# Loading two neighbouring input chunks by one transfer in a convolution with max pooling

## The chip, the core and the metric

The kernel runs on one core of a Trainium2 chip. The core has five engines that run side by side: TensorE (PE, matrix products), VectorE (DVE), ScalarE (ACT), GpSimd (POOL) and SyncE (SP, which in this kernel issues transfers and does no arithmetic). Sixteen DMA engines move data between the chip's large memory and the core's own memory; a transfer is issued by one instruction on SP, ACT or POOL, and raises a semaphore when it has landed. The metric is the device time of one execution in microseconds (us).

## The reference: a 3x3 convolution and a 2x2 maximum

The input `x` holds 16 images of 64 channels and 64 x 64 pixels, the weight is 128 x 64 x 3 x 3, everything in 32-bit floats. With the border padded by zeros:

```
conv[b, co, i, j] = sum over ci, kh, kw of weight[co, ci, kh, kw] * x_pad[b, ci, i+kh, j+kw]
output[b, co, i, j] = max of conv[b, co, 2i:2i+2, 2j:2j+2]
```

The output is 16 x 128 x 32 x 32.

## The kernel before

**Tiling.** Two images make a pair: their 64 channels each fill the 128 partitions. There are eight pairs, and each pair's 64 rows are cut into four chunks of 16 rows (eight pairs of rows, which is what the pooling takes together). That makes 32 chunks. The string `SEQ` gives each chunk one of two ways of being computed:

- 13 K chunks (names with `k`, and the step names in capitals): their input is loaded by POOL's queue, cast to bf16 on the way (`kload`, line 105, tile `kx`). One helper row tile `ks` is made for a chunk.
- 19 W chunks (names with `w`, step names in small letters): their input is loaded as 32-bit floats by SP's queue (`wload`, line 113) into one of three buffers `wx` that hold a whole pair of images each. From it four row tiles of sums and differences of rows are made on DVE and POOL by `row_op` (line 260): `we`, `ws`, `wz`, `wy`, steps `E`/`e`, `S`, `Z`, `Y`.

The matrix products (line 202) read `kx` and the row tiles and add into eight PSUM banks `acc`. ACT copies or negates banks (`ev` line 290, seeding line 295, `od` line 303), DVE takes the maxima (`acc` line 299, `o` line 327), and the finished chunk `o` of both images is stored from SP's queue (line 344). For the last two chunks the halves are stored one by one (lines 342 and 320), and of the last two such halves ACT issues one and SP the other (`flush_late`).

**Where chunks lie.** Chunks W16, W17 and W18 are the second, third and fourth quarter of the last pair of images; the first quarter of that pair is the last K chunk. All three lie in the buffer `wx_1`, which W4 to W7 have used before: W16 in its rows 15 to 32 of the image, W17 in rows 33 to 48, W18 in rows 49 to 63.

**Order.** Nothing is scheduled by a program: the string `ORDER` (lines 420 to 477) is the issue order, read from left to right, and each engine executes its own instructions in that order. `LD.16`, `LD.17` and `LD.18` are the loads of the three chunks. `LD.16` and `LD.17` stand on line 454; `LD.18` stands ten lines further on, on line 464, ahead of `e.17`. The steps that read W17's rows are `e.17` (POOL), `S.17` (DVE), `Z.17` and `Y.17`; those that read W18's are `S.18`, `e.18`, `Y.18`, `Z.18`. `L4` on line 453 is a K load on POOL's queue that is in flight beside `LD.16` and `LD.17`. SP executes loads and stores in the same order, so a store that waits for its data holds up every later transfer of SP.

**Semaphores.** The transfers issued by SP and ACT take eight semaphores in turn, the first transfer the first of them, the ninth the first again, and so on. There are 57 such transfers, so the last one, the store of line 320 on SP, takes the first semaphore, and the store of line 320 on ACT, one before it in the order, takes the eighth. At the end of the program SP waits for the eight semaphores one after the other, from the first to the eighth; these instructions, and the barrier of all engines behind them, show under line 543.

Of the kernel before, what the change touches and what calls it, by code (L numbers as in the profile page):

```python
# [10 lines left out]
def kernel(  # L11
# [31 lines left out]
    place = {}  # L43
    number = {}
    for c in SEQ.lower():
        i = sum(1 for g in place if g[0] == c)
        j, q = divmod(i, NQ)
# [25 lines left out]
    def behind(inst, other):  # L73
        if other is not None:
            tc.add_manual_dep(inst.ins, other.ins.name, SYNC, reason="order")
# [9 lines left out]
    def rows_of(p, lo, hi):  # L85
        return x[2 * p : 2 * p + 2].rearrange("b c h w -> (b c) h w")[:, lo:hi, :]

    def chunk(q):
        return (2 * R * q + (q > 0), min(H, 2 * R * (q + 1) + 1))

    kx = {}
    loaded = set()
# [11 lines left out]
        hi = chunk(q + n - 1)[1]  # L104
        return nc.gpsimd.dma_start(out=ktile(i)[:, lo:hi, :], in_=rows_of(p, lo, hi))  # L105

    def wload(i):
        loaded.add(i)
        p, q = place["w", i]
        lo, hi = chunk(q)  # L110
        if i % NQ == 0 and q:
            lo -= 2
        return nc.sync.dma_start(
            out=wx[i // NQ % 3][:, lo + 1 : hi + 1, :], in_=rows_of(p, lo, hi)
        )
# [17 lines left out]
    D2, G0, D0, G2, GM, G1, GP = range(1, 29, 4)  # L133
# [118 lines left out]
    mark = {}  # L252
# [33 lines left out]
    ev, od, ot = {}, {}, {}  # L286
# [80 lines left out]
    def load_second():  # L367
        return nc.sync.dma_start(out=ksecond, in_=rows_of(0, klo2, khi2))

    def load_w(i):  # L370
        behind(wload(i), mark.get({0: "D2", 1: "GM", 2: "E0", 3: "E1"}.get(i)))

    def note(name, inst):
        mark[name] = inst
# [4 lines left out]
    def load_k(n):  # L379
# [21 lines left out]
        "X2": lambda e: cast_more(e, 1),  # L401
        "KX2": lambda: behind(load_second(), mark["D2"]),
        "LD": load_w,
        "L": load_k,
        "KS": lambda i: note(f"KS{i}", ks(i)), "S": ws, "Z": wz, "Y": wy, "SE": seed,
# [6 lines left out]
    for name, f in ("ev", evac), ("mx", rowmax), ("od", odd), ("cm", colmax):  # L412
# [38 lines left out]
        mx.9.1 P2.10.0:2+PR.7.1 SE.10.1:1 cm.7.0 PBb.7.0+P1.9.1 E.11 OD.7.1 P1.9.0+P0.10.1 LD.14 CM.7.1  # L451
        od.9.1 Z.12 MX.7.0 LD.15 PAa.8.0:4+P3.10.1 od.9.0 cm.9.1 ev.10.1 PR.7.0+PAa.8.1:6 S.11 SE.10.0:3
        PAb.8.0+PAb.8.1 Y.11 mx.10.1 OD.7.0 P3.10.0+P2.11.1:0 CM.7.0 EV.8.1 cm.9.0 P0.10.0+P1.10.1 L4 KS.8
        SE.11.1:6 S.12 PBa.8.0:7+PBa.8.1:5 ev.10.0 LD.16 E.12 PBb.8.0+P0.11.1 EV.8.0 LD.17 mx.10.0 od.10.1
        Y.13 P2.11.0:2+PBb.8.1 ev.11.1 MX.8.0 P1.10.0+P3.11.1 SE.11.0:4 cm.10.1 Y.12 PR.8.0+PAa.9.1:0 MX.8.1
        od.10.0 P0.11.0+P2.12.1:1 mx.11.1 OD.8.0 Z.13 cm.10.0 P3.11.0+PR.8.1 ev.11.0 CM.8.0
        P2.12.0:3+P1.11.1 OD.8.1 mx.11.0 e.13 SE.12.1:2 PBa.9.0:7+PAb.9.1 CM.8.1 od.11.1 P1.11.0+P3.12.1
# [3 lines left out]
        CM.9.1 OD.9.0 Y.15 ev.13.1 CM.9.0 P1.13.0+P2.14.1:0 od.12.1 mx.13.1 od.12.0 PAa.11.0:4+P2.15.1:5  # L461
        od.13.0 Z.15 cm.12.0 SE.14.1:7 PAb.11.0+P1.13.1 cm.12.1 cm.13.0 PAa.10.0:6+P0.14.1 od.13.1 E.16
        SE.15.1:1 PAb.10.0+P3.14.1 S.15 ev.14.1 P2.14.0:2+P0.15.1 EV.11.0 cm.13.1 S.14 L5 P2.15.0:0+P3.15.1
        ev.15.1 LD.18 e.17 mx.14.1 PBa.10.0:4+PAa.11.1:3 EV.10.0 mx.15.1 SE.14.0:5 PBb.10.0+PAb.11.1
        SE.15.0:6 S.17 P0.14.0+P1.14.1 EV.11.1 KS.10 P0.15.0+P1.15.1 Z.17 MX.10.0 ev.14.0 P3.15.0+PAa.10.1:3
        od.15.1 ev.15.0 cm.15.1 P3.14.0+PAb.10.1 Y.16 od.14.1 mx.15.0 PR.10.0+PBa.10.1:2 EV.10.1 mx.14.0
        Y.17 P2.17.0:0+PBb.10.1 OD.10.0 cm.14.1 P1.15.0+P2.16.1:3 SE.17.0:1 MX.10.1 Z.16 P1.14.0+PAa.12.1:7
# [12 lines left out]
    for n in range(8):  # L480
        src = zeros if n > 5 else ones
        warm = nc.tensor.matmul(  # L482
            acc[:, n], src[:, 0:128], src, start=True, stop=True, skip_group_check=True
        )
        if n == 3:
            behind(load_second() if SEQ[1] == "K" else wload(0), warm)
# [6 lines left out]
    for s in ORDER.split():  # L493
        act_left[0] -= on_act(s)
        if s[0] == "P":
            made = []
            for p in s.split("+"):
                p, _, bank = p.partition(":")
                n, i, h = p.split(".")
# [48 lines left out]
```

## Time and profile before

| | us |
|---|---|
| time, median of 3 runs | 105.21 |
| lowest and highest | 104.98, 105.22 |
| time of the profiled execution | 104.99 |
| its span, first to last instruction | 103.1 |
| PE busy | 97.3 (94%) |
| DVE busy | 90.4 (88%) |
| ACT busy | 81.8 (79%) |
| POOL busy | 67.2 (65%) |

Times inside the profile are counted from the start of the span. A name with a small q (SPq, POOLq, ACTq) is an engine's instruction sequencer: it issues transfers and waits for semaphores, and is not counted as busy. "DMA to landing" is the time from the issue of a transfer until its semaphore is complete. In rows of instructions the three durations are minimum, median and maximum in nanoseconds, and behind them stands when the first and the last instruction started. The time lies 1.9 us above the span in the profiled execution (104.99 - 103.1).

### The profile page before, as it was taken

How to read it: one execution, taken by the hardware profiler on the slowest of the kernel's cores; microseconds unless marked ns; L12 is line 12 of the kernel's file. 1: busy time of each engine (PE TensorE's matmuls, PEld its weight loads, DVE VectorE, ACT ScalarE, POOL GpSimd, SP SyncE). 2: the span in 40 equal slices, each digit the busy share in tenths (PEclk: the TensorE clock that was granted, in tenths of full speed). 3: DMA queues.
4: the chain of work that ended last, by engine and by line, in shares of the span. 5: the costliest groups of instructions: out<-in, count | busy, mean ns of one | idle time of the engine just before them, and what ended most of it. 6: DMA issues, size and time to landing. Idle time of an engine off the chain costs nothing.

```text
span 103.1 us, 2507 instructions
## 1 busy us (share of the span) xinstructions
PE 97.3 (94%) x888; PEld 57.3 (56%) x888; DVE 90.4 (88%) x178; ACT 81.8 (79%) x177; POOL 67.2 (65%) x76
## 2 busy tenths in 40 slices
PE   6998999999999999999999999999999999999920
PEld 2273555555765555655555665665555656666500
DVE  1599979998898898897998999989999999989950
ACT  4478987787988867799879988889889988988630
POOL 7306679847958769967795856993992697580000
PEclk9999999999999999999999999999999999999999
DMA  2987988899998996689899788999947921512362
GB/s 52 366 287 246 211 174 284 208 302 224 373 354 283 153 231 261 227 216 147 189 284 416 269 189 301 270 217 267 358 155 154 244 114 68 197 43 97 108 230 79
DMA packets 12925, 22.81 MB, mean 221 GB/s; under 512 B 1008, under 2 KB 9200, under 8 KB 12912
## 3 DMA queue, kind: packets, MB, share of 16 engines
q1 hardware_dynamic: 11904, 19.63, 57.5%
q0 software_dynamic: 864, 2.88, 19.2%
q8 instruction: 7, 0.11, 0.5%
q10 hardware_dynamic: 144, 0.13, 0.4%
q14 instruction: 6, 0.05, 0.1%
HBM read 17.14 MB, written 8.39 MB: 248 GB/s over the span
## 4 chain that ended last, share of the span: by engine, by line
PE 81%; DMA 7%; DVE 5%; issue 1%; ACT 1%
PE acc L202 81%; DMA ksecond<-in_x_dram 5%; DMA wraw<-in_weight_dram 3%; DVE acc L299 2%; DVE o L327 2%; DVE wq L391 1%; ACT kx L348 1%; DVE wq L356 0%
## 5 line engine op out<-in xcount | busy, mean ns | idle before, releaser
L202 PEld LDWEIGHTS <-wt 64*128 64x128 bf16 x852 | 54.6, 94 | 36.8 <-issue 0.6
L202 PE MATMUL acc<-kx,wt 64*128 64x504 bf16 (+5 forms) x318 | 57.5, 369 | 0.3 <-ACT kx L348 0.3
L299 DVE TENSOR_TENSOR acc<-acc,ev 128x512 f32<-128x512 f32 x64 | 42.4, 692 | 3.1 <-PE acc L202 2.0
L290 ACT COPY ev<-acc 128x512 f32<-128x512 f32 x64 | 36.6, 592 | 6.2 <-PE acc L202 5.5
L260 POOL TENSOR_TENSOR wz<-wx 128x512 bf16<-128x512 f32 x19 | 24.2, 1275 | 10.6 <-DVE ks L260 4.3
L202 PE MATMUL acc<-wy,wt 64*128 64x504 bf16 (+1 forms) x114 | 29.6, 377 | 0.0
L260 POOL TENSOR_TENSOR wy<-wx 128x512 bf16<-128x512 f32 x19 | 24.1, 1273 | 7.8 <-PE acc L202 3.1
L202 PE MATMUL acc<-wz,wt 64*128 64x504 bf16 (+1 forms) x114 | 29.2, 377 | 0.0
L202 PE MATMUL acc<-we,wt 64*128 64x504 bf16 (+1 forms) x114 | 29.1, 377 | 0.0
L202 PE MATMUL acc<-ws,wt 64*128 64x504 bf16 (+1 forms) x114 | 29.1, 376 | 0.0
L327 DVE TENSOR_TENSOR o<-acc,od 128x256 f32<-128x256 f32 x64 | 25.2, 417 | 2.3 <-ACT od L303 1.9
L303 ACT COPY od<-acc 128x256 f32<-128x256 f32 x64 | 23.0, 381 | 4.1 <-PE acc L202 3.2
L295 ACT ACTIVATE acc<-acc 128x512 f32<-128x512 f32 x38 | 22.0, 586 | 3.3 <-DVE o L327 1.9
L202 PE MATMUL acc<-ks,wt 64*128 64x504 bf16 (+1 forms) x78 | 19.5, 377 | 0.0
L260 POOL TENSOR_TENSOR we<-wx 128x512 bf16<-128x512 f32 x11 | 14.0, 1271 | 5.1 <-PE acc L202 3.4
L260 DVE TENSOR_TENSOR ws<-wx 128x512 bf16<-128x512 f32 x19 | 15.0, 793 | 0.0
L260 DVE TENSOR_TENSOR we<-wx 128x512 bf16<-128x512 f32 x8 | 6.1, 768 | 0.0
L260 DVE TENSOR_TENSOR ks<-kx 128x512 bf16<-128x512 bf16 x13 | 5.4, 419 | 0.1
L105 POOL DMA_DIRECT2D kx<-in_x_dram x6 | 3.5, 592 | 0.0
L482 PE MATMUL acc<-const-bfloat16-1.0 128*128 128x512 bf16 x6 | 2.7, 623 | 0.8 <-PEq L529 0.8
L356 DVE TENSOR_TENSOR wq<-wraw 128x192 bf16<-128x192 f32 x1 | 0.5, 502 | 2.6 <-DMA wraw<-in_weight_dram 2.6
L164 PEld LDWEIGHTS <-wq 128*128 128x128 bf16 x28 | 1.7, 101 | 1.6 <-issue 0.9
(28 smaller groups left out, 18.5 us busy)
## 6 DMA issues: line engine op xcount, KB each, us to landing
out_dram<-o SPq DMA_DIRECT2D x30, 256.0 KB, 4.7
wx<-in_x_dram SPq DMA_DIRECT2D x9, 512.0 KB, 7.2
wx<-in_x_dram SPq DMA_DIRECT2D x5, 480.0 KB, 6.0
wx<-in_x_dram SPq DMA_DIRECT2D x4, 544.0 KB, 6.6
kx<-in_x_dram POOLq DMA_DIRECT2D x3, 496.0 KB, 8.0
kx<-in_x_dram POOLq DMA_DIRECT2D x2, 528.0 KB, 8.6
wx<-in_x_dram SPq DMA_DIRECT2D x1, 576.0 KB, 9.7
ksecond<-in_x_dram SPq DMA_DIRECT2D x1, 512.0 KB, 4.7
```

The source lines that it names most:

```text
L105: return nc.gpsimd.dma_start(out=ktile(i)[:, lo:hi, :], in_=rows_of(p, lo, hi))
L164: nc.tensor.transpose(turned_rows(m)[:, j, :], wq[:, BLOCKS[m] - 1 + j : BLOCKS[m] + 1 + j, :].rearrange("a b c -> a (b c)"), ident,)
L202: lambda kw=kw, o0=o0, o1=o1, c0=c0, c1=c1: nc.tensor.matmul(dst[:, i0:i1, o0:o1], wt[lo : lo + CI, m0 + kw - h, :], rows(lo, i0, i1, c0, c1),
L260: return engine.tensor_tensor(out=r, in0=t[:, f + a : f + a + 2 * R - 1 : 2, :], in1=t[:, f + b : f + b + 2 * R - 1 : 2, :], op=op,)
L290: nc.scalar.copy(out=ev[g], in_=acc[:, ta[g]])
L295: nc.scalar.mul(acc[:, t], acc[:, ta["w", i, h]], -1.0)
L299: nc.vector.tensor_tensor(out=t, in0=t, in1=ev.pop(g), op=MAX)
L303: nc.scalar.copy(out=od[g], in_=acc[:, tb[g], :, 1::2])
L327: nc.vector.tensor_tensor(out=o[:, h], in0=acc[:, tb[g], :, 0::2], in1=od.pop(g), op=MAX,)
L348: nc.scalar.copy(out=out, in_=in_)
L391: "D2", on_vector(nc.vector.tensor_sub(out=slots(D2), in0=g2, in1=g1))
L482: warm = nc.tensor.matmul(acc[:, n], src[:, 0:128], src, start=True, stop=True, skip_group_check=True)
```

## The change

`wload` and the step `LD` take a second number, how many neighbouring chunks of one pair of images are to be loaded by one transfer. `LD.17` becomes `LD.17.2`: one transfer of rows 33 to 63, 992 KB, 7936 bytes in each partition, at the place of the old `LD.17`. `LD.18` is taken out of its place on line 464. The instructions of PE, DVE, ACT and POOL stay as they are and in their order. On SP and ACT 56 transfers are left in place of 57, and each transfer that follows the removed one takes the semaphore before the one that it had; the last store takes the eighth in place of the first, and the last store of ACT the seventh in place of the eighth.

```diff
-    def wload(i):
-        loaded.add(i)
+    def wload(i, n=1):
+        loaded.update(range(i, i + n))
         p, q = place["w", i]
-        lo, hi = chunk(q)
+        assert place["w", i + n - 1] == (p, q + n - 1)
+        lo, hi = chunk(q)[0], chunk(q + n - 1)[1]
         if i % NQ == 0 and q:
             lo -= 2
         return nc.sync.dma_start(
...
-    def load_w(i):
-        behind(wload(i), mark.get({0: "D2", 1: "GM", 2: "E0", 3: "E1"}.get(i)))
+    def load_w(i, n=1):
+        behind(wload(i, n), mark.get({0: "D2", 1: "GM", 2: "E0", 3: "E1"}.get(i)))
...
-        SE.11.1:6 S.12 PBa.8.0:7+PBa.8.1:5 ev.10.0 LD.16 E.12 PBb.8.0+P0.11.1 EV.8.0 LD.17 mx.10.0 od.10.1
+        SE.11.1:6 S.12 PBa.8.0:7+PBa.8.1:5 ev.10.0 LD.16 E.12 PBb.8.0+P0.11.1 EV.8.0 LD.17.2 mx.10.0 od.10.1
...
-        ev.15.1 LD.18 e.17 mx.14.1 PBa.10.0:4+PAa.11.1:3 EV.10.0 mx.15.1 SE.14.0:5 PBb.10.0+PAb.11.1
+        ev.15.1 e.17 mx.14.1 PBa.10.0:4+PAa.11.1:3 EV.10.0 mx.15.1 SE.14.0:5 PBb.10.0+PAb.11.1
```

## The prediction

> **What bounds the kernel now.** I read the page first, then the chain that ended last, then who waited for whom on PE and SP, then the end of the program, and last the transfers that the change touches.
>
> ```profile
> span 103.1 us, 2507 instructions
> PE 97.3 (94%) x888; PEld 57.3 (56%) x888; DVE 90.4 (88%) x178; ACT 81.8 (79%) x177; POOL 67.2 (65%) x76
> ```
>
> The chain that ended last (start, duration, what), its long middle and its end:
>
> ```profile
> 10.36 83.77 PE acc L202 x772
> 94.12 0.60 DVE acc L299
> ...
> 98.38 1.09 DVE o L327 x3
> ```
>
> PE runs without a break for 83.8 us and sets the pace from 10.4 to 94.1 us. Behind it comes a tail of DVE and stores. In the middle, time can be lost only by something that makes PE wait, and PE hardly waits: the only wait of its products is 0.3 us in total.
>
> ```profile
> PE acc L202 <- ACT kx L348: 0.3, 1, 0.3
> ```
>
> So a transfer that comes earlier can bring nothing there, and one that comes later costs something only when it comes later than its first reader. The tail is another matter: each instruction there stands on the path. The last stores, and what SP then waits for:
>
> ```profile
> L342 SPq DMA_DIRECT2D out_dram<-o x2: 408/413/418, 98.6 to 99.1; - x2
> ...
> L320 ACTq DMA_DIRECT2D out_dram<-o x1: 372/372/372, 99.2 to 99.2; - x1
> L320 SPq DMA_DIRECT2D out_dram<-o x1: 407/407/407, 99.6 to 99.6; - x1
> ...
> DMA to landing us min/median/max: 2.1/2.2/2.2
> ```
>
> ```profile
> SPq L344 <- DVE o L327: 62.3, 26, 6.3
> ...
> SPq L543 <- DMA out_dram<-o: 1.8, 1, 1.8
> ```
>
> The last store is issued at 99.6 and lands 2.2 us later, at 101.8. SP's waits show one wait of 1.8 us on line 543 for a store, 100.0 to 101.8, and no second one. The rows of SP's semaphore instructions on line 543 tell which of the eight that was; the first row takes the stretch 101.7 to 102.3, the second 101.81 to 101.82, the third 102.24 to 102.25, the fourth 102.3 to 102.33:
>
> ```profile
> L543 SPq EVENT_SEMAPHORE  x8: 17/28/28, 101.8 to 102.2; - x8
> ...
> L543 SPq EVENT_SEMAPHORE  x1: 17/17/17, 101.8 to 101.8; - x1
> ...
> L543 SPq EVENT_SEMAPHORE  x1: 28/28/28, 102.2 to 102.2; - x1
> ...
> L543 SPq DRAIN  x1: 7/7/7, 102.3 to 102.3; - x1
> ```
>
> All eight waits start after the last landing: the first of them is the one that the last store held up, and the seven others, long fulfilled, are worked off one by one behind it. From the first to the eighth it takes 0.42 to 0.44 us, some 62 ns for each of seven steps. Only then does SP drain and let the final barrier begin. Nothing else is late there.
>
> **The change, part by part.**
>
> *The last store's semaphore.* One transfer fewer stands ahead of it, so the rotation of eight moves back by one: the last store takes the eighth semaphore, ACT's store the seventh. The order of the end waits stays. SP is then through with issuing at 100.0 (99.6 + 0.4); the stores of line 342 land by 101.3 (99.1 + 2.2) and ACT's at 101.4 (99.2 + 2.2), so the first seven waits are worked off before the last landing at 101.8, with 0.3 us to spare after the seventh (101.4 + 0.06 = 101.5). At 101.8 the eighth alone is left. The steps from first to eighth, 7 x 62 ns = 0.43 us, leave the path and nothing fills the place: drain and barrier come 0.43 us earlier. Bounds: if only the 28 ns that each row records counted without a profiler, 7 x 0.028 = 0.20; from the first wait to the drain it is 0.50 (102.31 - 101.81), and more cannot go. I take 0.43, what this stretch itself measures.
>
> [...]
>
> *The merged load.* The old loads W16 and W17, then W18 (issue, and time to landing), with the rate at which W17 ran out:
>
> ```profile
> L113 SPq DMA_DIRECT2D wx<-in_x_dram x2: 446/598/751, 63.5 to 64.1; - x2
> ...
> DMA to landing us min/median/max: 9.7/10.0/10.3
> ```
>
> ```profile
> L113 SPq DMA_DIRECT2D wx<-in_x_dram x1: 468/468/468, 79.5 to 79.5; - x1
> ...
> DMA to landing us min/median/max: 5.0/5.0/5.0
> ```
>
> ```profile
> 72.00:74.00 2.00, 2.00 (x21) 1.14 (x18) 2.00 (x5) 1.76 (x4) 2.00 (x3) 1.00 1.01 375
> ```
>
> W17 landed at 74.4 (64.1 + 10.3). The 480 KB of W18 now ride with it. At the 375 GB/s of 72 to 74 us, where the DMA engines are full (share 1.01), 0.492 MB take 1.3 us; the other end is the whole 5.0 us that W18 took by itself. The merged transfer lands at 75.7, at the latest at 79.4. I take 75.7, since it follows W17 in the same queue without a new issue. A gain against 74.4 is excluded: there are more bytes in front of the same semaphore. First readers: POOL's `we` for W17, DVE's `ws` for W18; the first two rows below are DVE's `we` for W16 and the first product that reads the K load of step L4.
>
> ```profile
> 76.91 1.20 DVE L260 TENSOR_TENSOR we<-wx 128x512 bf16<-128x512 f32 x1
> ```
>
> ```profile
> L202 PE MATMUL acc<-kx,wt x7: 376/377/377, 75.5 to 76.8; 64*128 64x504 bf16 x4, 64*128 64x512 bf16 x3
> ```
>
> ```profile
> 79.88 1.26 POOL L260 TENSOR_TENSOR we<-wx 128x512 bf16<-128x512 f32 x1 [1.81 <-PE acc L202]
> ```
>
> ```profile
> 86.83 0.79 DVE L260 TENSOR_TENSOR ws<-wx 128x512 bf16<-128x512 f32 x1
> ```
>
> POOL's `we` starts at 79.88, and until then it waited for PE (a row buffer), not for the load. Cover 5.5 us, of which 1.3 are used; even 5.0 fit. `ws` of W18 starts at 86.83 with no idle time before it, so the old landing at 84.5 (79.5 + 5.0) cost nothing and the earlier one brings nothing. W16 stands ahead of the merged transfer in its queue and doesn't move. Cost: 0.
>
> *Stores behind it on SP.* The three stores issued at 67.5 to 71.5 stand in the same queue behind the merged transfer and land 1.3 us later (5.0 at most).
>
> ```profile
> L344 SPq DMA_DIRECT2D out_dram<-o x3: 372/395/395, 67.5 to 71.5; - x3
> ...
> DMA to landing us min/median/max: 4.9/6.7/7.6
> ```
>
> ```profile
> 82.63 0.43 DVE L327 TENSOR_TENSOR o<-acc,od 128x256 f32<-128x256 f32 x1
> ```
>
> The first of them landed at 75.1 (67.5 + 7.6), and its buffer `o`, one of six, is written again at 82.63. Cover 7.5 us. Cost: 0. SP itself is not late: even if the issue of the merged transfer took twice W17's 0.75 us it would be over at 65.6, and SP's next store is issued at 67.5.
>
> *What is taken away at 79.5.* SP loses one issue of 0.47 us and one semaphore wait. SP's stores waited 62.3 us in 26 waits for DVE, up to 6.3 us at a time, so this is worth 0. The waits of `ws` and `e.18` for W18's own semaphore go too: a few tens of ns on DVE, which is behind PE there. 0.
>
> *Sum.* Profiled execution: 104.99 - 0.43 + 0 = 104.56. The median of the runs shown is 105.21, 0.22 above the profiled execution. The same step off the median: 105.21 - 0.43 = 104.78, my forecast, 0.41% below. About 0.3% (0.32 us) is what a measurement of this kernel can tell from no change.
>
> **The rivals.**
>
> *A. The end shift is smaller than the profile makes it.* If the steps cost only the recorded 28 ns without the profiler, the gain is 0.20 and the time 105.01, within 0.3%. For it: a profiled sequencer may be slowed by being recorded. Against it: the profiled execution took 104.99, no more than the lowest of the runs, 104.98.
>
> *B. The merged load holds up the K load beside it, and PE waits: slower.* L4 was issued by POOL at 62.9:
>
> ```profile
> L105 POOL DMA_DIRECT2D kx<-in_x_dram x1: 570/570/570, 62.9 to 62.9; - x1
> ...
> DMA to landing us min/median/max: 10.2/10.2/10.2
> ```
>
> It landed at 73.1, and PE reads it at 75.5. Cover 2.4 us, the thinnest in this change, and on the engine that bounds. The rival decides from 2.4 us of delay on. With W18's own 5.0 us the load would land at 78.1 and PE would wait 2.6: 105.21 - 0.43 + 2.6 = 107.4. Against it: W16 landed at 73.2 (63.5 + 9.7), so L4 was in by the time that W17's bytes had the queue, and W18's come behind those. If all 1.3 us fell on L4, it would still land at 74.4. [...]
>
> *C. Nothing moves.* If the final barrier were held by another engine, or the end waits came in another order, the time would be 105.21. Against it: SP's drain follows the eighth wait within 0.1 us, and the other engines' last work, the stores aside, ends with DVE at 99.5 (98.38 + 1.09).
>
> **How the numbers follow.** Forecast 74%; A 12%, C 7%, together the 19% within 0.3%; B 7%. The forecast's margin over the bound is thin, 0.43 against 0.32, so I leave some of the "same" chance to scatter of the runs (0.24 from lowest to highest). Faster 0.74, same 0.19, slower 0.07. The range: below, the lowest run with the 0.50, 104.98 - 0.50 = 104.48, rounded down to 104.45; above, A's 105.01 with some scatter, 105.15. It leaves out B, C and a little of the rest, under 2 in 10.
>
> **What would show it.** In the profile after: SP's semaphore instructions on line 543, seven of them before the last landing and one behind it, the drain within 0.1 us of that landing, and a span of 102.7 (103.1 - 0.43). The chain keeps some 83.8 us of PE, PE has no new wait, and POOL's `we` near 79.9 still waits for PE. One load of 992 KB is issued at 64.1 and lands near 75.7. The prediction is wrong if PE waits for a `kx` load near 75.5, if POOL waits for `wx` near 79.9, or if several waits still stand behind the last landing.

## The result and the profile after

| | before | changed |
|---|---|---|
| time, median of 9 runs (us) | 105.20 | 104.53 |
| lowest and highest | 104.79, 105.57 | 104.31, 105.06 |
| profiled execution, time | 104.99 | 105.06 |
| its span | 103.1 | 103.2 |

The ratio, an estimate from all 18 runs and not the quotient of the medians, is 0.9952, with a 95% interval from 0.9928 to 0.9975: the changed kernel is faster by 0.50 us (0.0048 x 105.2), between 0.26 and 0.76. The forecast of 0.43 lies inside. The medians alone lie further apart, by 0.67 us. Ratios here and below are of fast runs; two of e7's ten runs, over 1.5% above its fastest, count as slow and are left out.

The profiled execution of the changed kernel happened to be its slowest run, and its span is no shorter than the one of before (the median span of its nine runs is 102.8). Whoever compared the two profiled spans would see nothing; the rows at the end show it. Shown are SP's waits, then its semaphore instructions on line 544 (line 543 before; every line from 114 on has moved by one). The first two rows of the second block take the stretch 100.4 to 102.4, the third row 101.88 to 101.92, the fourth 102.31 to 102.33; the third block holds the last two stores:

```profile
SPq L345 <- DVE o L328: 62.3, 25, 6.8
...
SPq L544 <- DMA out_dram<-o: 1.5, 4, 0.5
```

```profile
L544 SPq EVENT_SEMAPHORE  x8: 17/28/28, 100.5 to 102.3; - x8
L544 SPq DRAIN  x1: 7/7/7, 102.4 to 102.4; - x1
...
L544 SPq EVENT_SEMAPHORE  x1: 28/28/28, 101.9 to 101.9; - x1
...
L544 SPq EVENT_SEMAPHORE  x1: 28/28/28, 102.3 to 102.3; - x1
```

```profile
L321 ACTq DMA_DIRECT2D out_dram<-o x1: 371/371/371, 99.6 to 99.6; - x1
...
L321 SPq DMA_DIRECT2D out_dram<-o x1: 407/407/407, 100.0 to 100.0; - x1
...
DMA to landing us min/median/max: 2.3/2.3/2.3
```

The eight waits spread from 100.5 to 102.3 in place of 101.8 to 102.2: where there was one wait of 1.8 us for a store and seven waits behind it, there are now four waits that stores hold up, none longer than 0.5 us. The seventh starts at 101.9, when ACT's store has landed (99.6 + 2.3), the eighth at 102.3 with the last landing (100.0 + 2.3), and the drain comes within 0.1 us. The same is seen in the time from the end of the last maximum, the last row of the chain, to the end of the span:

```profile
98.84 1.09 DVE o L328 x3
```

It took 3.6 us before (103.1 - 98.38 - 1.09) and takes 3.3 us now (103.2 - 98.84 - 1.09), the last digit being rounded.

The merged load and its neighbours, in this order: the merged load with W16's load (the longer landing time is the merged one's, the shorter W16's), L4, POOL's first reader, and PE's waits:

```profile
L114 SPq DMA_DIRECT2D wx<-in_x_dram x2: 383/424/466, 64.1 to 64.6; - x2
...
DMA to landing us min/median/max: 8.6/9.6/10.7
```

```profile
L105 POOL DMA_DIRECT2D kx<-in_x_dram x1: 570/570/570, 63.4 to 63.4; - x1
...
DMA to landing us min/median/max: 7.2/7.2/7.2
```

```profile
80.31 1.26 POOL L261 TENSOR_TENSOR we<-wx 128x512 bf16<-128x512 f32 x1 [1.80 <-PE acc L203]
```

```profile
PE acc L483 <- PEq L530: 0.8, 1, 0.8
```

The merged transfer landed at 75.3 (64.6 + 10.7), POOL's `we` read it at 80.3 and had waited for PE as before, and PE's only listed wait is the one at its start. So no wait for the load shows.

Where the span's missing 0.43 us went is to be seen too. Counted by products, PE was 0.03 us behind the kernel before up to 65.1 us, and 0.46 us behind it from the next product on:

```profile
65.14 0.38 PE L203 MATMUL acc<-kx,wt 64*128 64x504 bf16 x1
65.60 0.37 PE L203 MATMUL acc<-ws,wt 64*128 64x512 bf16 x1
```

In the kernel before, this `ws` product started at 65.14. The chain shows what PE waited for here, a maximum of DVE:

```profile
64.86 0.70 DVE acc L300
65.56 0.04 issue
65.60 28.98 PE acc L203 x264
```

That maximum started at 64.32 in the kernel before. DVE had lost the half microsecond on one instruction (first before, then changed):

```profile
60.73 0.83 DVE L260 TENSOR_TENSOR ws<-wx 128x512 bf16<-128x512 f32 x1
```

```profile
60.76 1.35 DVE L261 TENSOR_TENSOR ws<-wx 128x512 bf16<-128x512 f32 x1
```

It began almost 4 us before the merged load was issued at 64.6, the first instruction in which the two kernels differ, so the load can't be its cause. POOL's `wz` ran beside it, 1.27 us long (1.28 before), and started at 60.28 in place of 59.73; in both kernels `ws` ended 0.55 to 0.56 us after the end of that `wz`. That POOL's instruction held up DVE's is suggested by this, not shown. In the run taken once more (the first experiment) this hole is absent: its chain has PE without a break from 16.5 to 94.4.

### The profile page after: what moved, and what is told of

Same layout as the page of the kernel before. It is cut to its first block, busy times and chain, and to the rows that moved or that the text cites. A ratio compares the mean times of both kernels' runs of the same rounds, so it can differ in the third digit from the quotient of the medians.

```text
span 103.2 us, 2506 instructions
## 1 busy us (share of the span) xinstructions
PE 98.1 (95%) x888; PEld 55.2 (53%) x888; DVE 90.8 (88%) x178; ACT 81.7 (79%) x177; POOL 67.1 (65%) x76
## 4 chain that ended last, share of the span: by engine, by line
PE 86%; DVE 6%; DMA 3%; issue 1%; DVEq 0%
PE acc L203 84%; DMA wraw<-in_weight_dram 3%; DVE acc L300 3%; PE acc L165 2%; DVE o L328 2%; DVE wq L392 1%; DVE wq L357 0%; DVE we L261 0%; DVEq L300 0%
## 5 line engine op out<-in xcount | busy, mean ns | idle before, releaser
L203 PEld LDWEIGHTS <-wt 64*128 64x128 bf16 x852 | 52.1, 94 | 39.4 <-issue 1.3
## 6 DMA issues: line engine op xcount, KB each, us to landing
wx<-in_x_dram SPq DMA_DIRECT2D x1, 992.0 KB, 10.7
```

The lines of the kernel that those rows point to most:

```text
L203: lambda kw=kw, o0=o0, o1=o1, c0=c0, c1=c1: nc.tensor.matmul(dst[:, i0:i1, o0:o1], wt[lo : lo + CI, m0 + kw - h, :], rows(lo, i0, i1, c0, c1),
```

## The experiments

Theory S is the prediction's: the gain is the place of the last store's semaphore among SP's end waits. Theory T is its rival: the transfer itself helps, by one issue fewer or by W18 coming earlier. The first four kernels ran on one chip beside one set of 35 runs of the kernel before, the last four on another beside another 35. The column before the ratio is worked out from the records of each profiled execution, to the hundredth: from the landing of the store that lands last to SP's drain behind the eight waits.

| run | semaphore of the store that lands last | W17 and W18 | last landing to drain (us) | ratio to before | 95% interval |
|---|---|---|---|---|---|
| before | first | apart | 0.52 | 1 | |
| the result | eighth | merged | 0.08 | 0.9952 | 0.9928 to 0.9975 |
| e1, the changed kernel | eighth | merged | 0.08 | 0.9955 | 0.9934 to 0.9976 |
| e2 | first | merged | 0.52 | 0.9997 | 0.9981 to 1.0013 |
| e3 | eighth | apart | 0.08 | 0.9950 | 0.9926 to 0.9975 |
| e4 | eighth | apart, W14 and W15 merged | 0.08 | 0.9968 | 0.9952 to 0.9985 |
| e5 | fourth | apart | 0.33 | 0.9972 | 0.9952 to 0.9991 |
| e6 | seventh | merged with W16 | 0.14 | 0.9981 | 0.9955 to 1.0007 |
| e7 | first | merged, 2 MB ahead | 0.52 | 1.0077 | 1.0054 to 1.0100 |
| e8 | seventh (SP); ACT's, on the eighth, lands earlier | merged | 0.14 | 0.9979 | 0.9960 to 0.9997 |

The fourth column follows the second alone: 0.08 us for the eighth semaphore and 0.06 us more for each place before it, whatever was merged or added. The ratios are coarser, and alone they don't order the fourth, seventh and eighth place.

### The changed kernel once more

No edit.

> The changed kernel once more, for a second profile beside the others. Theory S (the gain is the place of the last store's semaphore in SP's end waits): 0.43 us under the kernel before, ratio 0.996; behind the last landing one wait starts and the drain follows within 0.1 us. Theory T (the gain comes from the merged transfer itself, one transfer fewer on SP and earlier W18): the same time, so this run alone does not tell them apart.

Measured: ratio 0.9955, that is 0.47 us. SP's waits show the same picture as in the first profile.

```profile
SPq L544 <- DMA out_dram<-o: 1.4, 4, 0.5
```

### The merged load with 57 transfers

```diff
+    tiny = const.tile([128, 8, W], FP32, name="tiny")
+
+    def load_tiny(n):
+        for j in range(n):
+            nc.sync.dma_start(out=tiny[:, j : j + 1, :], in_=rows_of(0, j, j + 1))
...
-        ev.15.1 e.17 mx.14.1
+        ev.15.1 TINY.1 e.17 mx.14.1
```

The diff is against the changed kernel.

> The merged load stays, and a load of 32 KB that nobody reads is issued at the old place of LD.18, so that there are 57 transfers again and the last store takes the first semaphore. Theory S: as the kernel before, ratio 1.000 (0.999 to 1.001 by its cause), eight waits behind the last landing, 0.43 us from the first to the eighth. Theory T: the gain stays, ratio 0.995 to 0.996.

Measured: ratio 0.9997. With the merged load in place and the last store back on the first semaphore, the gain is gone. SP's waits, and its semaphore instructions of 101.7 to 102.35 and the drain behind them:

```profile
SPq L551 <- DMA out_dram<-o: 1.8, 1, 1.8
```

```profile
L551 SPq EVENT_SEMAPHORE  x8: 17/28/28, 101.9 to 102.3; - x8
...
L551 SPq DRAIN  x1: 7/7/7, 102.4 to 102.4; - x1
```

One wait of 1.8 us and all eight behind the landing: the same end as in the kernel before. Theory T falls. The interval also bounds the effect of the merged load with the small one added: between a gain of 0.20 and a loss of 0.14 us.

### Two loads as before, 64 transfers

```diff
-        ev.15.1 LD.18 e.17 mx.14.1
+        ev.15.1 LD.18 TINY.7 e.17 mx.14.1
```

The diff is against the kernel before; `TINY` as above.

> The loads of W17 and W18 stay apart as before, and seven loads of 32 KB that nobody reads follow LD.18, where SP has 6 us of idle time; 64 transfers, the last store takes the eighth semaphore. Theory S: 0.43 us under the kernel before, ratio 0.996, one wait behind the last landing. Theory T: not faster than before, ratio 1.000 or above, since seven transfers are added and nothing is merged.

Measured: ratio 0.9950, the gain without the merge and with seven transfers more. One wait and the drain stand at the end (stretch 102.1 to 102.3):

```profile
L550 SPq EVENT_SEMAPHORE  x1: 28/28/28, 102.2 to 102.2; - x1
L550 SPq DRAIN  x1: 7/7/7, 102.3 to 102.3; - x1
```

### Another pair merged

```diff
-        ... LD.14 CM.7.1
+        ... LD.14.2 CM.7.1
-        od.9.1 Z.12 MX.7.0 LD.15 PAa.8.0:4+P3.10.1
+        od.9.1 Z.12 MX.7.0 PAa.8.0:4+P3.10.1
```

`LD.17` and `LD.18` stand as in the kernel before; the step `LD` takes the number as in the change.

> W17 and W18 are loaded apart as before; W14 and W15 are loaded by one transfer in place of two; 56 transfers, the last store takes the eighth semaphore. Theory S: 0.43 us under the kernel before, ratio 0.996, as long as W14 is not late. Theory T in the form that the place of W17 and W18 matters: ratio 1.000.

Measured: ratio 0.9968, a gain of 0.34 us with 0.43 inside its interval. The gain came without the merge of W17 and W18, with a count that ends at 56.

### Two loads as before, 60 transfers: a half dose

```diff
-        ev.15.1 LD.18 e.17 mx.14.1
+        ev.15.1 LD.18 TINY.3 e.17 mx.14.1
```

The diff is against the kernel before; `TINY` as above.

> W17 and W18 apart as before, three loads of 32 KB that nobody reads after LD.18: 60 transfers, the last store takes the fourth semaphore. Theory S, a half dose: four waits behind the one that the last landing ends, 0.25 us from the fourth to the eighth in the profile against 0.43 from the first, so 0.19 us under the kernel before, ratio 0.998. Theory T: 1.000.

Measured: ratio 0.9972 (0.29 us off 104.87), with the expected 0.998 inside the interval. The time alone doesn't tell this dose from the full one, whose ratios lie between 0.9950 and 0.9968. The profile does (SP's semaphore instructions of 101.47 to 101.8):

```profile
L550 SPq EVENT_SEMAPHORE  x5: 27/28/28, 101.5 to 101.7; - x5
L550 SPq DRAIN  x1: 7/7/7, 101.8 to 101.8; - x1
```

Five of the eight waits start from the last landing on: the fourth, which it held up, and four behind it. The drain comes 0.33 us after that landing, between the 0.52 and the 0.08 of the two ends.

### Three chunks by one transfer

```diff
-        ... LD.16 E.12 PBb.8.0+P0.11.1 EV.8.0 LD.17.2 mx.10.0 od.10.1
+        ... LD.16.3 E.12 PBb.8.0+P0.11.1 EV.8.0 mx.10.0 od.10.1
```

The diff is against the changed kernel.

> W16, W17 and W18 by one transfer of 1536 KB at the place of LD.16: 55 transfers, the last store takes the seventh semaphore. Theory S with the covers as predicted: W16 lands with the rest near 75.7 (73.2 and 2.6 us for 960 KB more at 375 GB/s), its first reader starts at 76.9, so nothing waits; one wait more than in the changed kernel behind the last landing, 0.37 us under the kernel before, ratio 0.9965. If the cover of W16 is thinner than the profile says, DVE waits for it near 77, and PE behind it: ratio 0.998 or more.

Measured: ratio 0.9981, an interval that holds the expected 0.9965 and no change alike; the time doesn't decide. The profile shows the covers as expected: the load of 1536 KB landed at 75.7 (63.4 + 12.3), where 75.7 had been worked out, and DVE's `we` of W16 started with no idle time before it.

```profile
L114 SPq DMA_DIRECT2D wx<-in_x_dram x1: 467/467/467, 63.4 to 63.4; - x1
...
DMA to landing us min/median/max: 12.3/12.3/12.3
```

```profile
76.78 1.18 DVE L261 TENSOR_TENSOR we<-wx 128x512 bf16<-128x512 f32 x1
```

Its end shows one wait more than the changed kernel's (stretch 101.7 to 101.85, the last landing at 101.7):

```profile
L544 SPq EVENT_SEMAPHORE  x2: 28/28/28, 101.7 to 101.8; - x2
L544 SPq DRAIN  x1: 7/7/7, 101.8 to 101.8; - x1
```

### Two megabytes ahead of the merged load

```diff
+    idle = const.tile([128, 62, W], FP32, name="idle")
+
+    def load_idle(n):
+        nc.sync.dma_start(out=idle, in_=rows_of(0, 0, 62))
...
-        ... EV.8.0 LD.17.2 mx.10.0
+        ... EV.8.0 IDLE.1 LD.17.2 mx.10.0
```

The diff is against the changed kernel.

> The changed kernel with a load of 1984 KB that nobody reads on SP's queue just ahead of the merged load, four times the bytes that the change added there; 57 transfers, the last store takes the first semaphore, so the end is as in the kernel before. 2.03 MB at 375 GB/s are 5.4 us: the merged load lands near 80.7 to 81. Covers as predicted: POOL's we starts up to 1 us later than 79.9, PE reads it at 83.9 and doesn't wait, L4 lands before 75.5: ratio 1.000 to 1.003. Rival B (the load beside it, L4, is held up): PE waits for kx near 75.5, up to 3 us, ratio up to 1.03.

Measured: ratio 1.0077, slower than the 1.003 that the covers allowed, and far from the 1.03 of rival B. The profile shows a third thing. L4 and the merged load, then the K load that comes after them, L5 (issued at 77.5), then PE at 85.5:

```profile
L105 POOL DMA_DIRECT2D kx<-in_x_dram x1: 567/567/567, 62.9 to 62.9; - x1
...
DMA to landing us min/median/max: 8.1/8.1/8.1
```

```profile
L114 SPq DMA_DIRECT2D wx<-in_x_dram x1: 412/412/412, 64.6 to 64.6; - x1
...
DMA to landing us min/median/max: 15.9/15.9/15.9
```

```profile
L105 POOL DMA_DIRECT2D kx<-in_x_dram x1: 570/570/570, 77.5 to 77.5; - x1
...
DMA to landing us min/median/max: 8.7/8.7/8.7
```

```profile
85.49 0.38 PE L203 MATMUL acc<-ws,wt 64*128 64x512 bf16 x1
86.24 0.39 PE L203 MATMUL acc<-kx,wt 64*128 64x512 bf16 x1 [0.36 <-DMA kx<-in_x_dram]
```

L4 landed at 71.0, earlier than in the kernel before (73.1), with four times the added bytes behind it. The merged load landed at 80.5, close to the 80.7 worked out. But L5, issued while that load and the stores behind it were still under way, took 8.7 us and landed at 86.2, just when PE went on reading. In the kernel before L5 took 5.3 us:

```profile
L105 POOL DMA_DIRECT2D kx<-in_x_dram x1: 570/570/570, 77.5 to 77.5; - x1
...
DMA to landing us min/median/max: 5.3/5.3/5.3
```

It landed there at 82.8 and was read from 85.3 on. The six stores that were issued behind the merged load in e7, from 67.6 to 79.1:

```profile
L345 SPq DMA_DIRECT2D out_dram<-o x6: 372/374/395, 67.6 to 79.1; - x6
...
DMA to landing us min/median/max: 7.7/11.1/14.8
```

So in this run a K load on POOL's queue took 3.4 us longer beside SP's late transfers and PE waited 0.36 us for it, much as rival B said, but the victim is L5, not L4. The next `ws` product, at 86.24 too, comes 0.75 us after the one at 85.49 in place of 0.21, which is a loss of 0.54 us.

A second, smaller hole lies ahead of it: PE's starts at 83.15 and 83.55 are 0.40 us apart in place of 0.18 (83.11 and 83.29 before). POOL's `we`, then DVE's `ks`, then PE:

```profile
80.78 1.82 POOL L261 TENSOR_TENSOR we<-wx 128x512 bf16<-128x512 f32 x1 [2.68 <-DMA wx<-in_x_dram]
```

```profile
81.40 1.49 DVE L261 TENSOR_TENSOR ks<-kx 128x512 bf16<-128x512 bf16 x1
82.81 0.69 DVE L300 TENSOR_TENSOR acc<-acc,ev 128x512 f32<-128x512 f32 x1
```

```profile
83.15 0.38 PE L203 MATMUL acc<-kx,wt 64*128 64x504 bf16 x1
83.55 0.37 PE L203 MATMUL acc<-ks,wt 64*128 64x512 bf16 x1
```

POOL's `we` waited for the merged load and started 0.9 us later than before; DVE's `ks` ran beside it and took 1.49 us in place of 0.41; the maximum behind `ks` ended at 83.50, and PE went on 0.05 us later. So PE did not wait for `we` (its only listed waits are 0.8 us at its start and 0.4 us for `kx`), but lost 0.2 us behind a `ks` that took 1.08 us longer beside the late `we`. Why `ks` was slow there was not tested. Counted by products, PE was 0.05 us behind the kernel before ahead of the first hole, 0.26 behind it after that hole and 0.80 after the second: the two together are most of the 0.81 us that the ratio gives (0.0077 x 104.87, interval 0.57 to 1.05).

### The last two stores swapped between the queues

```diff
-            queue = nc.scalar if stored["late"] % 2 else nc.sync
+            queue = nc.sync if stored["late"] % 2 else nc.scalar
```

The diff is against the changed kernel.

> The changed kernel with the last two stores swapped between the queues: the last but one is issued by SP (seventh semaphore), the last by ACT (eighth). SP's last issue now comes 0.09 us after its data are ready, since SP is busy with the store before; ACT is free. Expected: the last landing up to 0.1 us earlier, ratio to the kernel before 0.9945 to 0.996. If SP's second last store then lands last, nothing is gained.

Measured: ratio 0.9979, no better than the changed kernel's. Both stores are now issued at 99.9:

```profile
L321 ACTq DMA_DIRECT2D out_dram<-o x1: 393/393/393, 99.9 to 99.9; - x1
...
L321 SPq DMA_DIRECT2D out_dram<-o x1: 407/407/407, 99.9 to 99.9; - x1
```

SP's is issued no earlier than ACT's and lands 0.2 us later: 99.9 + 2.2 (102.16 by the records) against 99.9 + 2.1 (101.93). It is on the seventh semaphore, so the seventh and the eighth wait both stand behind the last landing (stretch 102.1 to 102.34):

```profile
L544 SPq EVENT_SEMAPHORE  x2: 28/28/28, 102.2 to 102.2; - x2
L544 SPq DRAIN  x1: 7/7/7, 102.3 to 102.3; - x1
```

This is the case that the expectation named, the store of SP landing last, and nothing is gained.

## Why the prediction was right, and where it was not

**The end waits.** The step that carries the forecast held as it was worked out. Its sum was 0.43; four measurements with the last store on SP and on the eighth semaphore (the result, e1, e3, e4) gave ratios of 0.9952, 0.9955, 0.9950 and 0.9968, that is 0.34 to 0.52 us. e2 and e3 decide it: the merge without the place brings no gain, the place without the merge brings it. The profiles give the size by itself: from the last landing to the drain 0.52 us with the first semaphore and 0.08 with the eighth, a difference of 0.43 us before rounding, and the steps between, 0.33 with the fourth and 0.14 with the seventh, fit the same 0.06 us a step. The absolute time, 104.53, lies 0.25 us under the forecast of 104.78: the medians moved by 0.67 us, more than the 0.50 that the prediction allowed the end waits, and what goes beyond it is scatter of the runs as far as the four ratios show.

**Rival A**, steps cheaper without a profiler, 0.20 us: the same four measurements all lie above it, and the lower ends of their intervals lie between 0.16 and 0.26 us. One of them alone leaves the rival open (e4); the four together speak against it, though three of them share one set of runs of the kernel before. Each run on record comes with a span and a clock of its own, so what a run without any recording takes is not shown.

**The merged load.** Its landing was put at 75.7 and was 75.3, partly by luck: it was issued at 64.6 and not at 64.1, and took 10.7 us in place of the 11.6 that the sum implies. Its cost was put at 0, and e2 measured 0.03 us of gain with no change inside the interval. No wait for the stores behind it shows either.

**What failed.** Two things, neither of which changed the result. The span was to be 102.7 and was 103.2, since PE lost 0.42 us at 65.1 in the profiled execution, by an instruction of DVE that ran before the change sets in; a span of one execution was too coarse a witness for 0.43 us. And rival B named L4 as the thinnest cover. e7 shows that L4, issued ahead of the added bytes, isn't touched (8.1 us, 10.2 before), while L5, issued 15 us later, is (8.7 us, 5.3 before): its cover of 2.5 us (82.8 to 85.3) is as thin, and what was late on SP's queue was still under way beside it. The prediction doesn't mention L5. In the changed kernel itself L5 was not late: it took 5.1 us. How SP's and POOL's queues share the DMA engines is not shown.

**Rival C**, nothing moves, is excluded by all intervals with the eighth semaphore.

## What to carry to other kernels

Look behind the last landing: here, waits for semaphores that were fulfilled long ago still cost 0.06 us each when the one that matters stood first among them, and the place followed from the number of SP's and ACT's transfers, so adding or removing one of them moved the end: the drain came 0.52 us after the last landing with 57 transfers and 0.08 us with 56. When a time changes after an edit to transfers, change the count back by a transfer that nobody reads before crediting the edit. And ask of a delayed queue which later load of another queue it will meet, not only which one is beside it: in e7 L5 took 8.7 us in place of 5.3.

## What the runs showed that was not expected

Single profiled executions lose time in different places of the middle or the start, also where the kernels don't differ. The chain of the changed kernel's second profile (e1) goes through a wait for an input load near its start, where the chain of the kernel before goes through `ksecond`; first e1, then the kernel before (start, duration, what):

```profile
6.72 5.45 DMA wx<-in_x_dram
```

```profile
4.99 4.67 DMA ksecond<-in_x_dram
```

Over nine runs the kernel before spread by 0.78 us (104.79 to 105.57), more than the whole gain; it took 9 to 12 runs of a changed kernel, and in the experiments 35 of the kernel before, to put a number on it. Beyond the one hole followed back above, what sets these holes was not studied.
